# Copying and accumulating the output projection's weight sums: each pair tied to an attention or retention norm, on GpSimd's queue

## The chip, the cores and the metric

The kernel runs on one core of a Trainium2 chip. The metric is device time in microseconds (us) of one execution. Before the change it is 1619.31 us, the median of 3 runs (1617.8 to 1620.54).

## What is computed

One layer of a decoder trunk for 256 tokens and 2048 channels, all in float32. Cut to what matters:

```python
h = rms_norm(x, ln1_g)
aq, ak, av, iq, ik, iw, rq, rk, rv, rg, ga, gb = split(h @ w_in)
o_attn = sparse_attention(rms_norm(aq), rms_norm(ak), av, top 64 keys by indexer(iq, ik, iw))
o_ret = silu(rg) * group_norm(retention(rotate(rq), rotate(rk), rv))
merged = sigmoid(ga) * (o_attn @ w_up_attn) + sigmoid(gb) * (o_ret @ w_up_ret)
x = x + merged @ w_out
x = x + square(relu(rms_norm(x) @ w_ff1)) @ w_ff2
```

Every weight is read once from HBM. The two norms that matter here are the head norms of `ak` and of the four parts of `aq`, and the group norms of the four parts of the retention.

## The kernel before

**Matrix products.** The weights come in blocks of 512 columns (368 for the indexer's), each block in parts of 4 x 128 rows: 1 MB for 512 columns. A part is loaded into one of four `raw` buffers (`load`, L380, SP's queue). `split_now` makes two pieces of each half of a part: a high one, `whi`, on ScalarE (L429) and the remainder, `wlo`, on VectorE (L430). `products` (L495 to L497) runs three matmuls per 128 rows and token tile: high by high, high by low, low by high. A half of a part is thus 12 matmuls, a part 24. A `raw` buffer comes free when the last `wlo` of its part is made, and only then is the next load issued on SP's queue.

**Order of the work.** `program()` lists all halves of parts in order: first `AK` and the indexer's block `I 0` together, then `I 1`, `I 2`, `AV`, four blocks `AQ`, two of `RV`, then the gates' blocks, then four blocks `RG` (the retention runs beside them), `UR`, the output projection and the feed-forward part. `weights()` moves on by one item and calls `ahead()`, which issues loads and splits for later items. Work that is not a weight product (indexer, norms, softmax, transposes) lies in Python generators that `step()` advances by one `yield` for every 128 rows of products. A scheduler then orders the instructions of each engine; the order is fixed when the program is built.

**Strassen's form and the sums in DRAM.** Some products are made by a seven-product scheme on quarters A, B, C, D of a weight matrix, which needs sums of quarters. For the output projection `w_out`, half of its weights are formed ahead of time in four DRAM tensors `pre`: A+B, B+C, C+(A+B) and D+(C+A+B). Each tensor has two halves of 1 MB, so there are eight pairs of DMAs: a **copy** of a quarter from the weights into `pre` (`nc.sync.dma_start`, L453, SP's queue), and an **accumulation** of the second quarter, or of an earlier `pre`, onto it (`accum_op=ALU.add`, L451, GpSimd's queue). The table `background` says at which item of `program()` each is issued: copies at items 22, 31, 40, 49, 58, 67, and the last two pairs at the first item of `RG` and nine later; the accumulation 8 items after its copy. The copies depend on nothing, so the scheduler was free to put them earlier. The first reader of `pre` is a load at L380 at 829.4 us.

**GpSimd's queue** (POOL in the profile) executes in order and holds: the power in `rsqrt` (L507) of every norm, the accumulations, the stores of the gates' results (`keep`, L793), accumulations into `raw` (L437), and in the retention the loads of its values (`rvs`, L970), of the group norm's gains (`mid`, L972) and of the stored gates (`got`, L994, L998). A DMA on it that has to wait for another DMA makes everything behind it on POOL wait.

**The norms.** `head_norm_T` makes the norm of a block: squares, sums, then `rsqrt`, which is a VectorE operation (L506) and a power on POOL (L507); after a `yield`, VectorE scales the rows. `retain` makes the retention of two heads, its statistics (L949, L950), then `rsqrt` and an offset `off` on VectorE (L954), and ScalarE normalizes with both (L959). `small` tiles are the few columns that hold such factors.

Of the kernel before, what the change touches and what calls it, by code (L numbers as in the profile page):

```python
# [14 lines left out]
ALU = mybir.AluOpType  # L15
# [3 lines left out]
D = 2048  # L19
# [13 lines left out]
KC, HC = 4, 2  # L33
# [79 lines left out]
HK = DK // 2  # L113
# [64 lines left out]
def program():  # L178

    out = [(z, h, s) for h in range(DK // KC) for s in range(KC // HC) for z in (("AK", 0), ("I", 0))]  # L180
    for key in [("I", 1), ("I", 2), ("AV", 0)] + [("AQ", i) for i in range(4)] + [("RV", 0), ("RV", 1)]:
        out += block(key)
    out += gates()
    for i in range(4):
        out += block(("RG", i))
    out += [(z, h, s) for h in range(DK // KC) for s in range(KC // HC) for z in (("UR", 0), ("UR", 1))]
    out += second_half()
    out += block(("F1", 1), NORM_COLS) + block(("F1", 0))
    for g in range(1, NG):
        out += merged(g)  # L190
    return out + [("F2", NG - 1, i, h, s) for i in range(D // BN) for h in F2_HALVES for s in range(KC // HC)]
# [17 lines left out]
def block_kernel(ctx, tc, cst, rot, xt, gains, w, x, ret_gn_g, ret_gn_b, out):  # L209
    nc = tc.nc  # L210
# [16 lines left out]
    def nm(s):  # L227
        uid[0] += 1
        return f"{s}_{uid[0]}"
# [20 lines left out]
    def small(w):  # L250
        return sp.tile([P, w], F32, tag="small", name=nm("small"), bufs=n_sm)
# [47 lines left out]
    at, B, base, off = {}, {}, {}, 0  # L299
# [12 lines left out]
    use = program()  # L312

    pre = {z: dp.tile([HK // KC, P, KC * BN + 16], F32, name=nm("pre"))[:, :, :KC * BN].rearrange("h p (c n) -> h p c n", c=KC) for z in QUARTERS}
    formed = set()
    for n, p in enumerate(OUT_ORDER):
        z = PRODUCTS[p][1]
        for h in range(HK // KC):
            at[("OQ", n), h] = (pre[z][h] if p in (1, 2, 4, 6) else base[z, h], BN)
    background = {}  # L320
    late_at = use.index((("RG", 0), 0, 0))
    paced = [22 + 9 * j for j in range(6)] + [late_at, late_at + 9]
    for j, (z, two) in enumerate((("A", "B"), ("B", "C"), ("C", "A"), ("D", "C"))):
        for h in range(HK // KC):
            i = paced[2 * j + h]
            background[i] = (pre[z][h], base[z, h], False)
            background[i + 8] = (pre[z][h], base[two, h] if j < 2 else pre[two][h], True)

    def tile_of(item):
        if item[0] == "Q" and item[1] == OUT:  # L330
            return ("OQ", item[2]), item[3]
        if item[0] == "Q":
            return (PRODUCTS[ORDER[item[2]]][1], item[1], item[3]), 0
        if item[0] == "F2":
            return item[:4], 0
        return item if item[0] in BESIDE else item[:2]
# [18 lines left out]
    next_load, next_split, now, quarter, second_w, n_second = [0], [0], [0], [0], [0], [0]  # L355

    def ring(key):
        if key in BESIDE:
            return 3
        return 2 if key[0] == "F2" and key[1] < NG - 1 else 0  # L360
# [41 lines left out]
    def split(i):  # L402
        if first_gate - 16 <= i <= last_gate or first_out - 4 <= i <= last_out + 6:
            with tc.high_priority(offset=AHEAD):
                split_now(i)
        else:
            split_now(i)
# [32 lines left out]
    def room(i):  # L440
        key = loads[i][0]
        if key[0] in QUARTERS and "f2" not in late:
            return False
        n = ring(key)
        return not n or ("rawc" in late and second_w[0] - (n_second[0] // HT if key[0] == "F2" else n_second[0]) < n)

    def ahead(i):
        if i in background:
            d, a, add = background[i]
            if add:  # L450
                nc.gpsimd.dma_start(d, a, accum_op=ALU.add)  # L451
            else:
                nc.sync.dma_start(d, a)  # L453
        for _ in range(2):
            while next_load[0] < len(loads) and first_use[next_load[0]] <= i + LOAD_AHEAD and room(next_load[0]):
                load(next_load[0])
                next_load[0] += 1
            while next_split[0] < min(len(use), i + SPLIT_AHEAD + ("f1" in late or "fourth" in late) + 1):
                n_second[0] += ring(tile_of(use[next_split[0]])[0]) > 0
                split(next_split[0])  # L460
                next_split[0] += 1
# [41 lines left out]
    def rsqrt(v, n, mul):  # L503

        a, y = small(n), small(n)
        nc.vector.tensor_scalar(a, v, mul, EPS, op0=ALU.mult, op1=ALU.add)  # L506
        nc.gpsimd.tensor_tensor(y, a, half[:, :n], op=ALU.pow)  # L507
        return y
# [55 lines left out]
    def head_norm_T(rows, dsts, g, wait):  # L564

        hs = small(4 * T)
        for t, a in enumerate(rows):
            sq = stage()
            nc.scalar.activation(sq, a, AF.Square)
            nc.vector.tensor_reduce(hs[:, 4 * t:4 * t + 4], sq.rearrange("p (h d) -> p h d", h=4), axis=AX.X, op=ALU.add)  # L570
        yield
        r = rsqrt(hs, 4 * T, 1.0 / HD)
        yield
        for t, a in enumerate(rows):
            av = a.rearrange("p (h d) -> p h d", h=4)
            nc.vector.tensor_tensor(av, av, r[:, 4 * t:4 * t + 4].unsqueeze(2).to_broadcast([P, 4, HD]), op=ALU.mult)
        for _ in range(wait):
            yield
        for t, a in enumerate(rows):
            pst = psum_t()  # L580
            for h in range(4):
                nc.tensor.transpose(pst[:, h * P:(h + 1) * P], a[:, h * P:(h + 1) * P], ident)
            src = pst.rearrange("p (h i) -> p h i", h=4)
            if dsts[t][0] is not None:
                nc.scalar.activation(dsts[t][0], src, AF.Copy, scale=g)
            if len(dsts[t]) > 1:
                hi, lo = dsts[t][1:]
                nc.scalar.activation(hi, src, AF.Copy, scale=g)
                nc.vector.scalar_tensor_tensor(lo, src, g, hi.bitcast(F32), op0=ALU.mult, op1=ALU.subtract)
            yield  # L590
# [289 lines left out]
    for item in gates():  # L880
# [14 lines left out]
        if key == "UA":  # L895
            for t in range(T):
                a = stage()
# [27 lines left out]
    def retain(j, sg, rv, gb):  # L925
        h0 = 2 * j
        yield
        for a in range(2):
            k, q = rkT[:, h0 + a], rqT[:, h0 + a]
            ps = psum_a()  # L930
            nc.tensor.matmul(ps[:, :S], k[:, :P], q, start=True, stop=True)
            nc.tensor.matmul(ps[:, S:S + P], k[:, P:], q[:, P:], start=True, stop=True)
            z = stage()[:, :S + P]
            nc.vector.tensor_tensor(z[:, :S], ps[:, :S], dec[:, h0 + a].rearrange("p b i -> p (b i)"), op=ALU.mult)
            nc.vector.tensor_tensor(z[:, S:], ps[:, S:S + P], dec[:, h0 + a, 0], op=ALU.mult)
            nc.scalar.activation(am[:, 0, a], z, AF.Copy)
            nc.vector.tensor_tensor(am[:, 1, a], z, am[:, 0, a].bitcast(F32), op=ALU.subtract)
            yield
        yield
        yield  # L940
        psy, mv = [psum_a() for _ in range(T)], small(4 * T)
        for t in range(T):
            for a in range(2):
                c = slice(a * RV, (a + 1) * RV)
                for n, (x, i) in enumerate(((0, 0),) if t == 0 else ((2, 1), (1, 0))):
                    products([psy[t][:, c]], [z[:, i, c] for z in rv], [[am[:, b, a, x * P:(x + 1) * P] for b in range(2)]], n == 0, n == t)
            for a in range(2):
                st = small(6)
                nc.vector.bn_stats(st, psy[t][:, a * RV:(a + 1) * RV])  # L949
                nc.vector.bn_aggr(mv[:, 4 * t + 2 * a:4 * t + 2 * a + 2], st)  # L950
            yield
        mean, var = (mv.rearrange("p (a b) -> p a b", b=2)[:, :, i] for i in range(2))
        r, off = rsqrt(var, 2 * T, 1.0), small(2 * T)
        nc.vector.scalar_tensor_tensor(off, mean, -1.0, r, op0=ALU.mult, op1=ALU.mult)  # L954
        for t in range(T):
            y = stage()
            for a in range(2):
                c, i = slice(a * RV, (a + 1) * RV), 2 * t + a
                nc.scalar.activation(y[:, c], psy[t][:, c], AF.Identity, bias=off[:, i:i + 1], scale=r[:, i:i + 1])  # L959
            yield  # L960
            nc.vector.tensor_tensor(y, y, gb[0], op=ALU.mult)
            nc.vector.tensor_tensor(y, y, gb[1], op=ALU.add)
            nc.vector.tensor_tensor(y, y, sg[t], op=ALU.mult)
            yield
            work.append(transpose_in(rT, 4 * j, t, y, W_GN))

    for j in range(4):
# [8 lines left out]
        for t in range(T):  # L976
            z = mid([P, BN])
# [331 lines left out]
```

## Time and profile before

| | before |
|---|---|
| Time, median of 3 runs | 1619.31 us |
| Profiled execution's own time | 1618.96 us |
| Its span | 1616.9 us |
| PE busy | 1597.2 us, 99% of the span, 7370 matmuls |
| PEld (weight loads of TensorE) busy | 1322.6 us |
| DVE busy | 1326.8 us |
| ACT busy | 1039.5 us |
| POOL busy | 131.1 us |
| Moved by DMA | 391.65 MB, mean 242 GB/s |

PE is TensorE's matmuls, PEld its weight loads, DVE VectorE, ACT ScalarE, POOL GpSimd, SP the SyncE, which only issues DMAs. All times are microseconds from the span's start. Matmuls overlap, so a row's duration is longer than the distance to the next start, and PE counts as busy nearly always; what a stall costs is read from the distance between starts. "DMA share" is the mean busy share of the core's 16 DMA engines; q1 is the queue of SP's DMAs, q0 that of GpSimd's. A DMA's "us to landing" runs from its issue to its completion. PEclk is the TensorE clock that was granted, as a share of full speed.

### The profile page before, as it was taken

Reading aid. Unit: us, or ns where it says so; the run is one execution under the profiler, and the core shown is the slowest. Engines: PE = TensorE matmul, PEld = TensorE weight load, DVE = VectorE, ACT = ScalarE, POOL = GpSimd, SP = SyncE. Lnnn points to the kernel's source line nnn. Section 1 sums busy time; section 2 is a strip of 40 time slices with the busy share of each in tenths; the row PEclk is TensorE's granted clock in tenths of the full one; section 3 lists DMA queues with packets and bytes.
Section 4 is the critical chain, followed back from the end, with each engine's and each line's share of the span. In section 5 each row is a group of like instructions: output and inputs, shape, how many; then the busy total and the mean of one; then the engine's idle time right before and its main releaser. Section 6 shows DMA issues by size and latency. Waiting matters only on the chain.

```text
span 1616.9 us, 19794 instructions
## 1 busy us (share of the span) xinstructions
PE 1597.2 (99%) x7370; PEld 1322.6 (82%) x7370; DVE 1326.8 (82%) x1380; ACT 1039.5 (64%) x1290; POOL 131.1 (8%) x177
## 2 busy tenths in 40 slices
PE   9998999999999999999999999999999999999998
PEld 8976888888888888888878878888888888888887
DVE  6576877989989899687777789898989898989884
ACT  6553657666767676454556786766777676767672
POOL 0100000100100000111110000010000000000000
PEclk9999999999999999999999999999999999999999
DMA  9999447979788684874767874768676777777773
GB/s 328 291 329 298 153 142 259 308 256 310 242 291 266 226 264 155 294 249 164 285 234 287 305 268 177 237 208 258 201 242 209 236 232 234 234 234 230 217 205 129
DMA packets 78928, 391.65 MB, mean 242 GB/s; under 512 B 8944, under 2 KB 15728, under 8 KB 42864
## 3 DMA queue, kind: packets, MB, share of 16 engines
q1 hardware_dynamic: 58240, 326.00, 55.0%
q0 software_dynamic: 17856, 58.21, 16.6%
q10 hardware_dynamic: 2736, 6.18, 1.0%
q8 instruction: 58, 0.95, 0.2%
q14 instruction: 38, 0.31, 0.0%
HBM read 360.99 MB, written 46.14 MB: 252 GB/s over the span
## 4 chain that ended last, share of the span: by engine, by line
PE 92%; DMA 3%; DVE 3%; ACT 1%; issue 1%; SPq 0%; DVEq 0%; ACTq 0%
PE pm L497 12%; PE pm L496 12%; PE pm L495 12%; PE pq L495 10%; PE pq L496 10%; PE pq L497 10%; PE pf L495 7%; PE pf L497 7%; PE pf L496 7%; DMA raw<-in_w_dram 3%; DVE wlo L430 1%; PE pt L524 1%; ACT whi L429 1%; PE pa L495 0%; PE pa L496 0%
## 5 line engine op out<-in xcount | busy, mean ns | idle before, releaser
L430 DVE TENSOR_TENSOR wlo<-raw,whi 128x1024 fp32r<-128x1024 f32 (+2 forms) x568 | 675.0, 1203 | 188.9 <-ACT whi L429 179.4
L429 ACT ACTIVATE whi<-raw 128x1024 fp32r<-128x1024 f32 (+2 forms) x568 | 587.8, 1042 | 371.0 <-PE pm L497 196.4
L495 PE MATMUL pm<-whi,act 128*128 128x512 f32 (+1 forms) x928 | 360.1, 389 | 6.0 <-ACT whi L429 6.0
L496 PE MATMUL pm<-wlo,act 128*128 128x512 f32 (+1 forms) x928 | 357.9, 386 | 2.9 <-DVE wlo L430 2.9
L497 PE MATMUL pm<-whi,act 128*128 128x512 f32 (+1 forms) x928 | 357.2, 385 | 0.0
L430 DVE TENSOR_TENSOR wlo<-rawc,whi 128x1024 fp32r<-128x1024 f32 x176 | 214.8, 1221 | 41.4 <-ACT whi L429 39.5
L429 ACT ACTIVATE whi<-rawc 128x1024 fp32r<-128x1024 f32 x176 | 186.6, 1060 | 84.8 <-PE pf L497 23.2
L495 PEld LDWEIGHTS pm<-whi,act 128*128 128x128 f32 x928 | 174.7, 188 | 39.0 <-ACT whi L429 7.9
L496 PEld LDWEIGHTS pm<-wlo,act 128*128 128x128 f32 x928 | 174.8, 188 | 36.8 <-DVE wlo L430 6.2
L497 PEld LDWEIGHTS pm<-whi,act 128*128 128x128 f32 x928 | 174.7, 188 | 32.8
L495 PE MATMUL pf<-whi,act 128*128 128x512 f32 x512 | 200.0, 391 | 0.2 <-ACT whi L429 0.2
L497 PE MATMUL pf<-whi,act 128*128 128x512 f32 x512 | 199.5, 390 | 0.0
L496 PE MATMUL pf<-wlo,act 128*128 128x512 f32 x512 | 199.3, 389 | 0.0
L417 DVE TENSOR_TENSOR raw<-raw,raw 128x2048 f32<-128x2048 f32 x86 | 196.6, 2286 | 0.8
L495 PE MATMUL pq<-whi,xf 128*128 128x512 f32 x416 | 163.6, 393 | 0.0
L496 PE MATMUL pq<-wlo,xf 128*128 128x512 f32 x416 | 162.2, 390 | 0.0
L497 PE MATMUL pq<-whi,xf 128*128 128x512 f32 x416 | 162.1, 390 | 0.0
L497 PEld LDWEIGHTS pf<-whi,act 128*128 128x128 f32 x512 | 96.1, 188 | 20.1
L495 PEld LDWEIGHTS pf<-whi,act 128*128 128x128 f32 x512 | 96.0, 188 | 20.1 <-ACT whi L429 0.6
L496 PEld LDWEIGHTS pf<-wlo,act 128*128 128x128 f32 x512 | 96.2, 188 | 19.9
L1255 POOL DMA_DIRECT2D sums<-ev x56 | 49.1, 967 | 577.5 <-ACT ev L1254 577.0
L497 PEld LDWEIGHTS pq<-whi,xf 128*128 128x128 f32 x416 | 78.1, 188 | 16.3
(223 smaller groups left out, 1718.8 us busy)
## 6 DMA issues: line engine op xcount, KB each, us to landing
raw<-in_w_dram SPq DMA_DIRECT2D x186, 1024.0 KB, 7.0
rawc<-in_w_dram SPq DMA_DIRECT2D x56, 1024.0 KB, 6.5
rawc<-in_w_dram SPq DMA_DIRECT2D x64, 512.0 KB, 5.9
sums<-ev POOLq DMA_DIRECT2D x56, 256.0 KB, 5.5
raw<-in_w_dram POOLq DMA_DIRECT2D x10, 1024.0 KB, 9.8
pre<-in_w_dram SPq DMA_DIRECT2D x8, 1024.0 KB, 18.5
raw<-pre SPq DMA_DIRECT2D x8, 1024.0 KB, 5.7
raw<-in_w_dram SPq DMA_DIRECT2D x8, 736.0 KB, 6.1
```

Source lines behind the costliest of these rows:

```text
L417: nc.vector.tensor_tensor(one, one, two, op=ALU.add)
L429: nc.scalar.activation(a, src, AF.Copy)
L430: nc.vector.tensor_tensor(b, src, a.bitcast(F32), op=ALU.subtract)
L495: nc.tensor.matmul(d, h, hi, start=first, stop=False, skip_group_check=skip)
L496: nc.tensor.matmul(d, h, lo, start=False, stop=False, skip_group_check=skip)
L497: nc.tensor.matmul(d, l, hi, start=False, stop=last, skip_group_check=skip)
L524: nc.tensor.transpose(ps[:, c * P:(c + 1) * P], src[:, c * P:(c + 1) * P], ident)
L1255: nc.gpsimd.dma_start(sums[:, t, i * BN:(i + 1) * BN], z, accum_op=ALU.add)
```

## The change

The table of fixed places is replaced by a function `pace(mark)`, called at nine norms: right after `rsqrt` in `head_norm_T` (one call for `AK`, four for `AQ`), and after `off` in `retain` (four calls, of which the first three find a pair left). Each call takes the next of the eight pairs in the same order as before and issues on GpSimd's queue: a DMA of one element of the norm's result into the first element of the target in `pre`, then the copy of the quarter over the same target. Because both write the same bytes, the copy waits for the one-element DMA, and that one for the norm; so the scheduler can't put the copy earlier. The accumulation follows, again 8 items later in `program()` and on GpSimd's queue.

```diff
     background = {}
-    late_at = use.index((("RG", 0), 0, 0))
-    paced = [22 + 9 * j for j in range(6)] + [late_at, late_at + 9]
-    for j, (z, two) in enumerate((("A", "B"), ("B", "C"), ("C", "A"), ("D", "C"))):
-        for h in range(HK // KC):
-            i = paced[2 * j + h]
-            background[i] = (pre[z][h], base[z, h], False)
-            background[i + 8] = (pre[z][h], base[two, h] if j < 2 else pre[two][h], True)
+    pairs = [(z, two, h) for z, two in (("A", "B"), ("B", "C"), ("C", "A"), ("D", "C")) for h in range(HK // KC)]
+
+    def pace(mark):
+
+        if pairs:
+            z, two, h = pairs.pop(0)
+            d = pre[z][h]
+            nc.gpsimd.dma_start(d[0:1, 0, 0:1], mark[0:1, 0:1])
+            nc.gpsimd.dma_start(d, base[z, h])
+            background[now[0] + 8] = (d, base[two, h] if z in "AB" else pre[two][h])
...
     def ahead(i):
         if i in background:
-            d, a, add = background[i]
-            if add:
-                nc.gpsimd.dma_start(d, a, accum_op=ALU.add)
-            else:
-                nc.sync.dma_start(d, a)
+            d, a = background[i]
+            nc.gpsimd.dma_start(d, a, accum_op=ALU.add)
...
         r = rsqrt(hs, 4 * T, 1.0 / HD)
+        pace(r)
         yield
...
         nc.vector.scalar_tensor_tensor(off, mean, -1.0, r, op0=ALU.mult, op1=ALU.mult)
+        pace(off)
         for t in range(T):
```

The order of PE, DVE and ACT is the same in both programs, instruction for instruction. Lines of the changed program are numbered 2 or 3 higher below the table.

SP's queue in the indexer's blocks, where `raw` are the weight loads in their order of use and `pre_123` to `pre_126` are the sums of A, B, C and D. Before:

```order
L380 DMA raw_563<-in_w_dram 128x4x368
L453 DMA pre_123<-in_w_dram 128x2048
L380 DMA raw_597<-in_w_dram 128x4x368
L453 DMA pre_123<-in_w_dram 128x2048
L380 DMA raw_647<-in_w_dram 128x4x368
L380 DMA raw_685<-in_w_dram 128x2048
L453 DMA pre_124<-in_w_dram 128x2048
```

The same place of SP's queue with the change:

```order
L383 DMA raw_565<-in_w_dram 128x4x368
L383 DMA raw_599<-in_w_dram 128x4x368
L383 DMA raw_648<-in_w_dram 128x4x368
L383 DMA raw_686<-in_w_dram 128x2048
L383 DMA raw_721<-in_w_dram 128x2048
```

The eight copies have left SP's queue, and the weight loads stand there one behind the other.

POOL's queue in the attention, from the norm of `AK` (`small_536`) to that of the second `AQ` block. Before:

```order
L507 TENSOR_TENSOR small_536<-small_535,half 128x8
L451 DMA pre_123<-in_w_dram 128x2048 x2
L451 DMA pre_124<-in_w_dram 128x2048 x2
L451 DMA pre_125<-pre_123 128x2048 x2
L451 DMA pre_126<-pre_125 128x2048 x2
L507 TENSOR_TENSOR small_1331<-small_1330,half 128x8
L507 TENSOR_TENSOR small_1594<-small_1593,half 128x8
```

With the change (L328 is the one-element DMA, L329 the copy, L453 the accumulation):

```order
L507 TENSOR_TENSOR small_536<-small_535,half 128x8
L328 DMA pre_123<-small_536 1x1
L329 DMA pre_123<-in_w_dram 128x2048
L453 DMA pre_123<-in_w_dram 128x2048
L507 TENSOR_TENSOR small_1328<-small_1327,half 128x8
L328 DMA pre_123<-small_1328 1x1
L329 DMA pre_123<-in_w_dram 128x2048
L453 DMA pre_123<-in_w_dram 128x2048
L507 TENSOR_TENSOR small_1592<-small_1591,half 128x8
```

All eight accumulations stood ahead of the norm of the first `AQ` block; now one pair does, and one more follows each of the four `AQ` norms.

POOL's queue at the last pair, around the norm of the retention's third part (`small_6236`, with the change `small_6240`): `mid` are gains of the group norm, `got` the stored gates. Before:

```order
L972 DMA mid_6116<-in_ret_gn_g_dram 128x512
L972 DMA mid_6117<-in_ret_gn_b_dram 128x512
L507 TENSOR_TENSOR small_6236<-small_6235,half 128x4
L994 DMA got<-ga 128x512
L994 DMA got<-ua 128x512
```

With the change:

```order
L974 DMA mid_6120<-in_ret_gn_g_dram 128x512
L974 DMA mid_6121<-in_ret_gn_b_dram 128x512
L507 TENSOR_TENSOR small_6240<-small_6239,half 128x4
L328 DMA pre_126<-small_6243 1x1
L329 DMA pre_126<-in_w_dram 128x2048
L453 DMA pre_126<-pre_125 128x2048
L996 DMA got<-ga 128x512
L996 DMA got<-ua 128x512
```

A pair now stands between that norm and the loads of the stored gates; the norm of the fourth part (at 770.46 us in the profile before) comes behind them.

## The prediction

> **What bounds the kernel now.** I read the page first: its span and the line of DMA shares.
>
> ```profile
> span 1616.9 us, 19794 instructions
> DMA  9999447979788684874767874768676777777773
> ```
>
> The second line has 40 slices of 40.4 us. The first four are full, to about 160 us, and the next two at four tenths. So I asked for the busy times in stretches. Columns: stretch, its length, busy time of PE, PEld, DVE, ACT, POOL with instructions in brackets, granted clock, DMA share, GB/s.
>
> ```profile
> 50.00:78.00 28.00, 25.61 (x155) 25.01 (x155) 13.53 (x16) 12.24 (x18) 2.87 (x3) 1.00 0.99 301
> 78.00:110.00 32.00, 32.00 (x188) 26.30 (x188) 21.38 (x37) 18.64 (x27) 2.44 (x3) 1.00 1.02 356
> 110.00:142.00 32.00, 26.15 (x112) 19.30 (x109) 25.06 (x74) 11.47 (x15) 2.44 (x3) 0.98 1.02 297
> 160.00:255.00 95.00, 95.00 (x482) 78.91 (x481) 75.33 (x121) 61.23 (x127) 4.91 (x3) 1.00 0.41 145
> 680.00:765.00 85.00, 85.00 (x428) 72.19 (x427) 65.84 (x113) 40.92 (x56) 10.47 (x16) 1.00 0.56 198
> ```
>
> PE is full except in 50 to 142 us, where the DMA engines are full. The chain of waits passes there through two weight loads, one of 17.05 and one of 27.91 us (start, length, what):
>
> ```profile
> 57.88 17.05 DMA raw<-in_w_dram
> ...
> 76.86 0.44 PE pm L496
> ...
> 110.58 27.91 DMA raw<-in_w_dram
> ```
>
> What fills the engines, by the tile view of `pre` (median issue time, first and last start) and the DMA view (median us to landing; first of 110 to 140 us, then of 160 to 255 us):
>
> ```profile
> L453 SPq DMA_DIRECT2D pre<-in_w_dram x8: 496/530/621, 49.8 to 101.7; - x8
> L451 POOL DMA_DIRECT2D pre<-in_w_dram x4: 812/815/1065, 57.0 to 95.1; - x4
> L451 POOL DMA_DIRECT2D pre<-pre x4: 812/813/817, 107.6 to 136.5; - x4
> ```
> ```profile
> raw<-in_w_dram SPq DMA_DIRECT2D x4, 1024.0 KB, 22.1
> pre<-pre POOLq DMA_DIRECT2D x3, 1024.0 KB, 14.6
> ```
> ```profile
> raw<-in_w_dram SPq DMA_DIRECT2D x14, 1024.0 KB, 4.8
> ```
>
> All 16 transfers of `pre` are issued from 49.8 to 136.5 us. Beside them a weight load takes 22.1 us, without them 4.8. The timeline of PE shows where that reached it:
>
> ```profile
> 73.71 0.33 PE L497 MATMUL pm<-whi,act 128*128 128x368 f32 x1
> 75.90 0.43 PE L495 MATMUL pm<-whi,act 128*128 128x368 f32 x1 [1.86 <-ACT whi L429]
> ```
> ```profile
> 127.96 0.39 PE L496 MATMUL pm<-wlo,act 128*128 128x512 f32 x1
> 128.19 0.39 PE L497 MATMUL pm<-whi,act 128*128 128x512 f32 x1
> ...
> 130.97 0.50 PE L496 MATMUL pm<-wlo,act 128*128 128x512 f32 x1 [0.75 <-DVE wlo L430]
> ```
> ```profile
> 136.28 0.39 PE L497 MATMUL pm<-whi,act 128*128 128x512 f32 x1
> 139.70 0.50 PE L495 MATMUL pm<-whi,act 128*128 128x512 f32 x1 [3.04 <-ACT whi L429]
> 140.96 0.79 PE L496 MATMUL pm<-wlo,act 128*128 128x512 f32 x1 [0.76 <-DVE wlo L430]
> ```
> ```profile
> 140.80:144.20 3.40, 3.24 (x8) 2.56 (x9) 3.37 (x8) 2.93 (x5) 0.00 (x0) 0.50 1.01 277
> ```
>
> Matmuls of 512 columns start 0.23 us apart when nothing is missing (127.96, 128.19), those of 368 columns about 0.17. Three times PE waits for `whi` and then for `wlo` of a part that has just landed, and after the longest wait its clock is granted at 0.50 for 3.40 us (last row).
>
> **Part 1, the early stretch without seven of the pairs.** What stops there:
> - First stall: from 73.71 to 76.86 PE starts two matmuls, 3.15 us less 2 x 0.17 = 2.81 us.
> - Second: 128.19 to 130.97, 2.78 - 2 x 0.23 = 2.32 us. Third: 136.28 to 140.96, 4.68 - 0.46 = 4.22 us. Together 6.54.
> - Clock: 3.40 us at half speed, 1.70 us.
>
> If these waits go, VectorE is late next: in 110 to 142 it carries the indexer.
>
> ```profile
> 121.63 1.21 DVE L430 TENSOR_TENSOR wlo<-raw,whi 128x1024 fp32r<-128x1024 f32 x1
> 124.52 1.21 DVE L430 TENSOR_TENSOR wlo<-raw,whi 128x1024 fp32r<-128x1024 f32 x1
> 129.70 1.22 DVE L430 TENSOR_TENSOR wlo<-raw,whi 128x1024 fp32r<-128x1024 f32 x1 [2.19 <-ACT whi L429]
> 139.68 1.23 DVE L430 TENSOR_TENSOR wlo<-raw,whi 128x1024 fp32r<-128x1024 f32 x1 [4.16 <-ACT whi L429]
> ```
>
> Unhindered it makes a `wlo` every 2.89 us (121.63, 124.52), PE uses one up in 12 x 0.23 = 2.76. So PE stays behind VectorE there, and the second and third stall give back what VectorE idled, 2.19 + 4.16 = 6.35 us, not 6.54. The sum of part 1: 2.81 + 6.35 + 1.70 = 10.9 us (10.86).
>
> Does the first stall really go? Its load, issued at 57.88, had to share with copies and two accumulations; with the change, one copy and one accumulation are left from about 52 to 75 us. By the queue rows of 112 to 130 us (packets, MB, share of the 16 engines in 18 us) an accumulation costs 0.658 x 18 / 2.37 = 5.0 us of all engines per MB, a plain transfer 0.355 x 18 / 2.36 = 2.7:
>
> ```profile
> q0 software_dynamic: 321, 2.37, 65.8%
> q1 hardware_dynamic: 321, 2.36, 35.5%
> ```
>
> A pair is thus about 7.7 us of DMA time per MB, 8.1 for its 1.05 MB. Of the work ahead of that load at least one copy (2.8 us) and part of the second accumulation (5.3) leave, and it was late by 2.0 us (73.71 to 75.90, less 0.17). It lands in time, with some 4 us in hand.
>
> **Part 2, the seven pairs at their new places.** Four follow the `AQ` norms, three the retention's. POOL's timeline (start, length, operation, idle time ahead and its releaser) and who ends the quiet after:
>
> ```profile
> 147.77 1.66 POOL L507 TENSOR_TENSOR small<-small,half 128x8 f32<-128x8 f32 x1 [10.47 <-DVE small L506]
> 174.38 1.64 POOL L507 TENSOR_TENSOR small<-small,half 128x8 f32<-128x8 f32 x1 [24.95 <-DVE small L506]
> ```
> ```profile
> 738.40 1.03 POOL L507 TENSOR_TENSOR small<-small,half 128x4 f32<-128x4 f32 x1 [18.16 <-DVE small L506]
> 762.77 0.59 POOL L994 DMA_DIRECT2D got<-ga  x1 [23.34 <-PE pa L497]
> ```
> ```profile
> 770.46 1.18 POOL L507 TENSOR_TENSOR small<-small,half 128x4 f32<-128x4 f32 x1
> ```
>
> DMA time: 160 to 255 us is 0.41 x 95 = 39 us busy; four pairs add 32, in all 71 of 95. 680 to 765 is 0.56 x 85 = 48; three pairs add 24, in all 72 of 85. Both fit. A load may also be slow without harm: the one of 27.91 us stalled PE by 139.70 - 136.28 - 0.23 = 3.2 us, so one under some 24 us costs nothing in these blocks. With one pair in flight I expect 10 to 16. Taken: 0.
>
> POOL's own order: a pair holds POOL until its copy has landed, because the accumulation behind it waits. Nearest rows, for the one-element DMA the smallest one, for the copy one that SP issued in the quiet at 49.8 us and, as the upper end, the accumulations into `raw`, for the accumulation the first and the late ones (12.3, and 14.6 above):
>
> ```profile
> gT<-in_gains_dram ACTq DMA_DIRECT2D x1, 17.0 KB, 2.5
> ```
> ```profile
> pre<-in_w_dram SPq DMA_DIRECT2D x1, 1024.0 KB, 6.9
> ```
> ```profile
> raw<-in_w_dram POOLq DMA_DIRECT2D x10, 1024.0 KB, 9.8
> ```
> ```profile
> pre<-in_w_dram POOLq DMA_DIRECT2D x2, 1024.0 KB, 12.3
> ```
>
> POOL is held 2.5 + 6.9 to 9.8, some 10 to 12 us with the 0.81 us that an issue takes. The next `AQ` norm comes 174.38 - 147.77 = 26.6 us later, so nobody waits. At the last pair the norm starts at 738.40; its accumulation lands 1.03 + 2.5 + 6.9 + 12.3 = 22.7 us later, at 761, or at worst 1.03 + 2.5 + 9.8 + 14.6 = 27.9 later, at 766. The loads of the stored gates start at 762.77 on the same queue, and the fourth norm (770.46) stands behind them. So 0 to 4 us at the norm; since VectorE's and ScalarE's work lies between it and PE, I take 0.5. The issues themselves (16 one-element DMAs and copies x 0.81 = 13 us of POOL) lie in POOL's idle time. Less than nothing can't come from part 2: it only adds work.
>
> A rule that speaks against the change: the Trainium skill, "DMA: Bandwidth & Descriptors", section "Issuing engines are not separate DMA queues", says that DMAs from SP, ScalarE and GpSimd end on the same 16 engines and that another issuing engine saves only issue time. By it alone, moving the queue would be worth SP's issue time, and all else must come from the later time. This case's rows for q0 and q1 agree, since both share the same percentages.
>
> **The sum.** 1618.96 (the profiled execution's own time, 2.06 more than its span) - 10.9 + 0.5 = 1608.6. The median of the runs is 0.35 above that execution: 1608.9. No change means within 0.2%, 3.2 us, about what a measurement of this kernel can tell.
>
> **The rivals.**
> - *The last pair delays the fourth retention norm* (16%). The accumulation lands at 766 rather than 761, the loads of the stored gates queue behind it, and PE waits for the transposes of the normalized rows. For it: little slack, 1.8 us between 761 and 762.77. Price 2 to 4 us: 1611 to 1613. The same would follow if VectorE kept POOL from issuing: three issues, each longer by up to a `wlo`, 1.2 us, are 3.6 us more, at the same price. Against that part: with VectorE 78% busy in 110 to 142 us (25.06 of 32), issues of L451 took 0.81 us, at most 1.07. The Trainium skill, "SBUF — State Buffer", section "SBUF: two separate sides", states such a mechanism: while VectorE runs a two-port operation, GpSimd can't write its DMAs' descriptors. The rows of L451 show no such hold-up.
> - *The first pair still holds the load of 73 us* (8%). It is the one pair that stays early. Then 2.8 us less gain: 1611.7.
> - *Slower: both halves of each pair squeeze the weights* (4%). Beside accumulations q1 moved 2.36 MB in 18 us, 0.131 MB per us; PE uses 1.05 MB in 24 x 0.23 = 5.5 us, 0.19. If copies on GpSimd's queue behaved so too, each pair would squeeze for 25 of 26.6 us, 1.5 MB or 8 us of PE. Four pairs make 32 us; the slack of a load covers 24 - 4.8 = 19, 13 remain. Three retention pairs: 24 - 19 = 5. 1608.6 + 18 = 1627. It decides once loads take over 24 us in these blocks. Against it: in 78 to 110 five copies and three accumulations ran in 32 us, and PE was full.
> - *The tie doesn't hold* (4%): the copies go out early anyway or the indexer's VectorE work takes the place of the stalls; the time stays within 3 us of 1619. Against it: the copy writes bytes that the one-element DMA wrote before it, and VectorE's idle rows above.
>
> **How the numbers follow.** The forecast itself has 68%: all stalls gone, nothing new beyond 0.5 us, 1607.2 to 1610.5. The low end, 1606.8, is 1608.9 less 0.5 and less the scatter of a median (1.5). The high end takes in the first two rivals: 1613. Together 92%, less some for sizes that I mis-set. Faster by over 0.2%: 0.68 + 0.16 + 0.08 = 0.92; within: 0.04; slower: 0.04.
>
> **What would show it.** In the changed profile: of the transfers of `pre` only one pair before 130 us; DMA share in 80 to 140 us at half or less; weight loads of about 5 us there; no idle time of PE over 0.5 us between 70 and 145 us; the clock at 1.00 throughout it. In the `AQ` blocks, DMA share near 0.75 and PE full. At the last pair, the first load of the stored gates no later against the third norm than 24.4 us (762.77 - 738.40). Wrong would be: a PE wait for `whi` in the `AQ` or `RG` blocks, a `pre` copy over 12 us, or a third retention norm's accumulation that lands more than 26 us behind it.

## The result and the profile after

The changed kernel takes 1608.61 us (median of 4 runs, 1606.32 to 1610.49) against 1618.67 us before (4 runs, 1617.8 to 1620.54): ratio 0.9936, interval 0.9918 to 0.9953. That is 0.64% faster; 1608.9 was forecast. The profiled execution took 1607.76 us.

From the page of the changed kernel, the span and the DMA share in 40 slices of 40.1 us:

```profile
span 1605.6 us, 19809 instructions
DMA  9847578978878675798767874767686767777763
```

The span is 11.3 us shorter. Slices three and four, full before, read four and seven; slices five and six, four before, read five and seven. The same bytes move at other times. The stretches, with the columns as in the prediction:

```profile
50.00:78.00 28.00, 28.00 (x172) 27.86 (x171) 16.06 (x18) 14.63 (x20) 2.78 (x4) 1.00 0.89 294
78.00:110.00 32.00, 32.00 (x186) 25.62 (x185) 22.22 (x43) 19.23 (x28) 0.00 (x0) 1.00 0.45 156
110.00:142.00 32.00, 31.84 (x139) 24.98 (x138) 29.63 (x76) 14.66 (x16) 2.27 (x2) 1.00 0.51 183
160.00:255.00 95.00, 94.13 (x470) 77.99 (x469) 73.38 (x111) 57.70 (x110) 13.17 (x16) 1.00 0.70 230
680.00:765.00 85.00, 85.00 (x420) 71.85 (x418) 65.81 (x109) 42.28 (x57) 18.97 (x29) 1.00 0.90 287
```

PE is full in 50 to 142 us but for 0.16 us, the clock stays at 1.00, and the DMA share there falls to about a half, where it was 1.02. The new places carry the load: 0.70 where it was 0.41, 0.90 where it was 0.56, and PE stays full in the second. (The 0.87 us that PE lacks in 160 to 255 is the wait at 246.28 below, which stood at 257.61 before, outside this stretch.)

The tile view of `pre`: one-element DMA, copy, and the accumulations of the first four and of the last four pairs, with the first and last start:

```profile
L328 POOL DMA_DIRECT2D pre<-small x8: 587/602/737, 50.9 to 728.5; - x8
L329 POOL DMA_DIRECT2D pre<-in_w_dram x8: 534/542/574, 54.0 to 732.4; - x8
...
L453 POOL DMA_DIRECT2D pre<-in_w_dram x4: 841/849/860, 61.1 to 204.1; - x4
L453 POOL DMA_DIRECT2D pre<-pre x4: 853/868/872, 232.8 to 738.2; - x4
```

The tie holds: the copies run from 54.0 to 732.4 us, where they ran from 49.8 to 101.7. The DMA view of 78 to 142 us, then of 160 to 260 us (KB each, median us to landing):

```profile
raw<-in_w_dram SPq DMA_DIRECT2D x11, 1024.0 KB, 4.8
```
```profile
raw<-in_w_dram SPq DMA_DIRECT2D x13, 1024.0 KB, 6.2
```

Weight loads in the indexer's blocks take 4.8 us (22.1 before). Beside one pair at a time, in the `AQ` blocks, they take 6.2.

**Where the 11.3 us came from.** PE's order is the same in both kernels, so one and the same matmul can be compared. The rows show the matmul that starts at 73.71 us before, the last one ahead of the first stall, and a late one of the attention, at 256.34 before, first in the changed kernel and then in the kernel before:

```profile
73.35 0.33 PE L497 MATMUL pm<-whi,act 128*128 128x368 f32 x1
...
116.17 0.39 PE L495 MATMUL pm<-whi,act 128*128 128x512 f32 x1
116.71 0.50 PE L496 MATMUL pm<-wlo,act 128*128 128x512 f32 x1 [0.16 <-DVE wlo L433]
...
245.01 0.40 PE L497 MATMUL pq<-mid,vv 128*128 128x512 f32 x1
246.28 0.50 PE L495 MATMUL pq<-mid,vv 128*128 128x512 f32 x1 [0.87 <-ACT mid L734]
```
```profile
256.34 0.40 PE L497 MATMUL pq<-mid,vv 128*128 128x512 f32 x1
```

73.71 - 73.35 = 0.36 us lie ahead of everything that the change touches; 256.34 - 245.01 = 11.33. So 10.97 us came between 73 and 256 us, and matmul by matmul all of it by 146 us. From there to the end the two run in step (11.3 of the spans), but for some 1.1 us that the changed kernel gains at 800 us and loses again by 940. The wait for `wlo` at 116.71 is the one small wait that is left in the indexer; before, it ended at 120.00.

The last pair, by POOL's timeline and the DMA view of 735 to 745 us:

```profile
727.01 1.03 POOL L507 TENSOR_TENSOR small<-small,half 128x4 f32<-128x4 f32 x1 [10.00 <-DVE small L506]
...
738.15 0.87 POOL L453 DMA_DIRECT2D pre<-pre  x1 [5.19 <-DMA pre<-in_w_dram]
751.38 0.59 POOL L996 DMA_DIRECT2D got<-ga  x1 [12.36 <-PE pa L497]
```
```profile
pre<-pre POOLq DMA_DIRECT2D x1, 1024.0 KB, 8.1
```

The accumulation lands 738.15 + 8.1 - 727.01 = 19.2 us behind its norm, and the loads of the stored gates start 24.4 us behind it, as before. The loads of the stored gates wait for PE there, not for the pair.

### The profile page after: what moved, and what is told of

Same layout as the page of the kernel before. It is cut to its first block, busy times and chain, and to the rows that moved or that the text cites. A ratio compares the mean times of both kernels' runs of the same rounds, so it can differ in the third digit from the quotient of the medians.

```text
span 1605.6 us, 19809 instructions
## 1 busy us (share of the span) xinstructions
PE 1595.3 (99%) x7370; PEld 1322.6 (82%) x7370; DVE 1326.0 (83%) x1380; ACT 1040.9 (65%) x1290; POOL 141.3 (9%) x193
## 4 chain that ended last, share of the span: by engine, by line
PE 95%; DVE 3%; ACT 1%; issue 0%; DMA 0%; SPq 0%; DVEq 0%; ACTq 0%
PE pm L496 13%; PE pm L497 13%; PE pm L495 13%; PE pq L496 10%; PE pq L497 10%; PE pq L495 10%; PE pf L495 7%; PE pf L497 7%; PE pf L496 7%; DVE wlo L433 1%; PE pt L524 1%; DVE mid L651 1%; ACT whi L432 0%; PE pa L495 0%; PE pa L496 0%
```

## The experiments

**Theory** as in the prediction: the gain is the later time, since the DMA engines were full from 50 to 142 us. **Rival**: the gain is the queue, since no copy stands ahead of a weight load on SP's queue any more. Each ratio is to the kernel before, measured beside it.

**Queue without time: all eight pairs at the norm of `AK`.**

```diff
         r = rsqrt(hs, 4 * T, 1.0 / HD)
-        pace(r)
+        if wait == 2 * W_NORM:
+            for _ in range(8):
+                pace(r)
...
-        pace(off)
```

The accumulations follow one item apart, 8 to 15 items later.

> All eight pairs at the early place, but on GpSimd's queue and tied to the norm of AK: the queue is the changed kernel's, the time nearly that of before. Theory (the gain is the later time, because the DMA engines are full from 50 to 142 us): no gain, 1616 to 1624 us, PE stalls between 70 and 160 us, DMA share near 1.0 there; POOL may hold the first AQ norm a little longer than before. Rival (the gain is that no copy stands in front of a weight load on SP's queue): 1612 us or less, the stalls mostly gone.

Measured: 1617.85 us, ratio 1.0007 (0.9997 to 1.0017): no gain. PE's timeline, two stretches, and the weight loads of 78 to 142 us:

```profile
73.59 0.32 PE L497 MATMUL pm<-whi,act 128*128 128x368 f32 x1
77.22 0.68 PE L495 MATMUL pm<-whi,act 128*128 128x368 f32 x1 [3.31 <-ACT whi L432]
```
```profile
80.00:90.00 10.00, 9.34 (x43) 8.23 (x42) 3.08 (x5) 4.44 (x7) 2.57 (x4) 0.82 1.01 367
110.00:142.00 32.00, 31.85 (x143) 24.56 (x142) 30.21 (x83) 14.12 (x17) 1.61 (x2) 1.00 1.03 282
```
```profile
raw<-in_w_dram SPq DMA_DIRECT2D x10, 1024.0 KB, 19.5
```

The total fits the theory, but the time is not lost where it was lost before, so that the totals agree is chance. Compared matmul by matmul with the changed kernel, PE loses 7.7 us up to 86 us: the first stall is longer than before, and the clock drops behind it (0.82 on average in 80 to 90). Some 3 us more go between 142 and 158 us, where PE waits for rows of the first `AQ` block (longest 0.80 us at 149.85 and 0.84 at 157.56, both for VectorE); what made those late is not shown. In 110 to 142 us, with the engines full (1.03) and loads at 19.5 us, PE is as full as in the changed kernel: the second and third stall of before are gone. Full engines alone didn't stall PE there, and for that stretch the run speaks for the rival.

**Time without queue: the copies tied, but on SP's queue.**

```diff
-            nc.gpsimd.dma_start(d, base[z, h])
+            nc.sync.dma_start(d, base[z, h])
```

> The changed kernel with the eight copies issued on SP's queue again, each behind the one-element DMA that ties it to its norm: the time is the changed kernel's, the queue that of before. Theory (time): as the changed kernel within 2 us, 1607 to 1611 us. Rival (queue): the gain goes, 1615 us or more, with weight loads that wait behind a copy on SP's queue.

Measured: 1607.24 us, ratio 0.9937 (0.9924 to 0.9950), the changed kernel's. With the later time the queue is worth nothing that can be measured.

**Only the accumulations late.** The copies stand in the old table on SP's queue; `pace` issues the one-element DMA and puts the accumulation 8 items later.

```diff
-            background[i + 8] = (pre[z][h], base[two, h] if j < 2 else pre[two][h], True)
+            pairs.append((pre[z][h], base[two, h] if j < 2 else pre[two][h]))
...
+            d, a = pairs.pop(0)
+            nc.gpsimd.dma_start(d[0:1, 0, 0:1], mark[0:1, 0:1])
+            background[now[0] + 8] = (d, a, True)
```

> Copies as before (SP's queue, early), only the accumulations tied to the norms; the one-element DMA here overwrites one element of each copied half, so one weight of each is not the quarter's. Theory, by the price per MB (5.0 us of all engines for an accumulation, 2.7 for a copy): the seven accumulations are two thirds of what filled the engines; with the eight copies and one accumulation left, 50 to 142 us is about 60% full, weight loads take 8 to 10 us and no stall is left: 1607 to 1611 us. Rival (the copies ahead of the loads on SP's queue did it): 1614 us or more.

Measured: 1608.24 us, ratio 0.9939 (0.9927 to 0.9951): the whole gain. Two stretches and the loads of 78 to 142 us:

```profile
78.00:110.00 32.00, 32.00 (x187) 25.66 (x186) 22.16 (x41) 19.54 (x29) 0.00 (x0) 1.00 0.92 360
110.00:142.00 32.00, 31.85 (x140) 24.96 (x139) 29.66 (x79) 14.53 (x17) 2.28 (x2) 1.00 0.53 190
```
```profile
raw<-in_w_dram SPq DMA_DIRECT2D x10, 1024.0 KB, 5.2
```

All eight copies still stand among the loads, and the loads take 5.2 us in the median, since by 110 us the copies are through (0.53 after it). Early on the engines were fuller than expected: 0.94 in 50 to 78 us and 0.92 in 78 to 110, where about 0.6 was said for the whole stretch. With the accumulations gone, at 5.0 us of all engines per MB against 2.7, the copies no longer reach the stretch of the second and third stall.

**No pairs at all.** `at[("OQ", n), h]` reads `base[z, h]` for every product, and the table `background` stays empty.

> No copies and no accumulations at all: the output projection reads single quarters where it should read sums of quarters, so that part of the computation is left out. It shows what the pairs cost at their new places. Theory (nothing, PE is full there): the changed kernel's time within 1.5 us, 1607 to 1609.5 us, so about 0.65% under before. Rival (the new places cost some us that the sum missed): 1605 us or less.

Measured: 1608.08 us, ratio 0.9939 (0.9927 to 0.9951). A kernel without one copy or accumulation is no faster than the changed one, so the pairs cost nothing that can be measured at their new places.

**No pair at the norm of `AK`.**

```diff
-        pace(r)
+        if wait != 2 * W_NORM:
+            pace(r)
```

> The changed kernel without the pair at the norm of AK: pairs one to four at the AQ norms, five to eight at the four retention norms. It shows what the one pair that stayed early costs. Theory (its weight load lands in time): the changed kernel's time within 1 us, 1607.5 to 1609.5 us. Rival (that pair still holds something up): 1606.5 us or less.

Measured: 1607.97 us, ratio 0.9941 (0.9927 to 0.9955). The one pair that stayed early costs nothing either.

**All eight pairs at the four `AQ` norms**, two at each, the second accumulation 12 items later.

```diff
-        pace(r)
+        if wait != 2 * W_NORM:
+            pace(r)
+            pace(r)
```

> All eight pairs at the four AQ norms, two at each. Measured in the changed kernel, four pairs took the DMA share in 160 to 255 us from 0.41 to 0.70, 6.9 us a pair; eight make 39 + 55 = 94 of 95 us. Theory (loads may take up to 24 us before PE waits): the engines are full but PE keeps most of its time, 1608 to 1613 us, loads of 10 to 20 us. Rival (PE stalls as soon as the engines are full, as it did early): 1615 us or more, with a clock that drops again.

Measured: 1609.38 us, ratio 0.9951 (0.9939 to 0.9964). The stretch of the `AQ` blocks, and the loads of 150 to 245 us:

```profile
160.00:255.00 95.00, 94.13 (x471) 78.00 (x470) 73.32 (x112) 58.12 (x111) 18.89 (x25) 1.00 0.96 298
```
```profile
raw<-in_w_dram SPq DMA_DIRECT2D x13, 1024.0 KB, 11.4
```

The engines are full (0.96), loads take 11.4 us, and PE is as full in this stretch as in the changed kernel. That is the second place where full engines stall nothing. They are not quite free: the time is 1.4 us above the kernel without the pair at `AK`, measured beside it (1607.97). In its profile, PE loses 1.6 us just behind the stretch (287.70 to 289.52, less 0.23), waiting for a `wlo`. VectorE is 3.8 us late there, against the changed kernel, after waits for `whi` of up to 5.0 us (2.9 in the changed kernel). (The 6.9 us a pair in this expectation is too low; the price is worked out again below.)

**The last three pairs at the third retention norm.**

```diff
-        pace(off)
+        if j == 2:
+            for _ in range(3):
+                pace(off)
```

The accumulations follow 8, 9 and 10 items later.

> The last three pairs all at the third retention norm, so that POOL and its queue are held until after the loads of the stored gates should start, and the fourth norm comes late. It sizes the first rival of the prediction. If that rival's mechanism is right: the last accumulation lands some 40 us behind the norm, the fourth norm comes 10 to 15 us later, and PE waits about as long less the slack: 1615 to 1623 us. If the work behind that norm has slack: under 1611 us.

Measured: 1619.98 us, ratio 1.0014 (1.0005 to 1.0023): the gain is gone, 11 us. POOL, VectorE and PE around it:

```profile
753.47 0.80 POOL L453 DMA_DIRECT2D pre<-pre  x1 [10.89 <-DMA pre<-pre]
...
770.80 1.18 POOL L507 TENSOR_TENSOR small<-small,half 128x4 f32<-128x4 f32 x1
```
```profile
767.52 0.69 DVE L1001 TENSOR_TENSOR got<-got 128x512 f32<-128x512 f32 x1 [13.94 <-DMA got<-ua]
768.13 1.22 DVE L433 TENSOR_TENSOR wlo<-raw,whi 128x1024 fp32r<-128x1024 f32 x1
```
```profile
759.54 0.39 PE L495 MATMUL pm<-whi,act 128*128 128x512 f32 x1
769.40 0.79 PE L496 MATMUL pm<-wlo,act 128*128 128x512 f32 x1 [9.47 <-DVE wlo L433]
```

The accumulations hold the queue, the loads of the stored gates land late, and VectorE stands 13.94 us at the product of those gates with a `wlo` queued behind it. PE waits 9.47 us for that `wlo`, and its clock is granted at 0.54 for the 3.40 us from 769.80. The fourth norm comes at 770.80 us, 12 us later than in the changed kernel (758.62), as expected, but PE's wait is not for it.

**Untied: the kernel before with its copies on GpSimd's queue.**

```diff
             else:
-                nc.sync.dma_start(d, a)
+                nc.gpsimd.dma_start(d, a)
```

> The kernel before with its copies moved to GpSimd's queue by one word, and no tie. The scheduler then puts seven of the eight pairs ahead of the first norm on POOL. If the tie is what carries the change: slower than before, by 40 us or more, because the first norm waits on POOL until pairs have landed while the DMA engines are full with the first loads. If the queue alone were worth something: faster than before.

Measured: 1661.28 us (2 runs), ratio 1.0269 (1.0249 to 1.0289). The first norm on POOL, and PE's waits of 0 to 110 us (total, times, longest):

```profile
90.16 0.72 POOL L507 TENSOR_TENSOR small<-small,half 128x2 f32<-128x2 f32 x1 [31.60 <-DVE small L506]
```
```profile
PE pm L495 <- ACT whi L429: 32.1, 8, 7.8
```

The copies start at 1.29 us and meet the first loads. PE waits 32.1 us for `whi`, and the clock is granted at 0.83 in 0 to 50 us and at 0.64 in 50 to 78; the norm comes at 90.16 us and not at 40.66 because its sums come late, not because POOL holds it (the row names VectorE). Of the two reasons expected, only the DMA load was shown.

**A refined theory.** After these runs the theory needed a change: PE waits where a weight load takes longer than its buffers give it, and not where the engines are full. Two kernels test that: seven (then five) pairs tied to the transposed query tiles of the indexer at 80 to 90 us. Of the calls at the norms only that of `AK` is left (with five, also those of the retention), and an accumulation whose item is taken goes to the next free one.

```diff
             nc.scalar.activation(iqT[:, c:c + 2, :], ps.rearrange("p (a s) -> p a s", a=2), AF.Copy)
+            for _ in range(2):
+                pace(iqT[:, c, :])
```

> One pair at the norm of AK as in the changed kernel, the other seven tied to the indexer's four transposed query tiles, at about 80 to 90 us, on GpSimd's queue. So the DMA engines are full in 80 to 142 us again, as before, but no copy stands in front of a weight load on SP's queue, and the load that is needed at 73 us meets one pair alone. First theory (the gain is the later time: full DMA engines stall PE): 1614 us or more. Refined theory (PE waits only where a weight load takes longer than its buffers give it, 15 us in the indexer's blocks and 24 us in the next ones; behind pairs on another queue it takes 18 to 22 us): no wait for whi between 78 and 142 us although the DMA share is near 1.0; what remains is POOL, which holds the first AQ norm until the accumulations are issued, 0 to 4 us: 1608 to 1613 us.

Measured: 1626.81 us, ratio 1.0050 (1.0037 to 1.0063): slower, above what the refined theory said. The number lies in the first theory's "1614 us or more", but not for its reason, as the rows show. A stretch, the loads of 78 to 142 us, POOL and PE:

```profile
110.00:142.00 32.00, 31.06 (x133) 23.97 (x131) 26.55 (x72) 14.07 (x16) 1.61 (x2) 1.00 1.02 314
```
```profile
raw<-in_w_dram SPq DMA_DIRECT2D x10, 1024.0 KB, 11.7
```
```profile
148.09 0.80 POOL L456 DMA_DIRECT2D pre<-pre  x1 [28.53 <-DMA pre<-pre]
155.57 0.81 POOL L456 DMA_DIRECT2D pre<-pre  x1 [6.68 <-DMA pre<-pre]
156.12 1.96 POOL L510 TENSOR_TENSOR small<-small,half 128x8 f32<-128x8 f32 x1
```
```profile
140.82 0.39 PE L500 MATMUL pm<-whi,act 128*128 128x512 f32 x1
158.95 0.66 PE L587 MATMUL pt<-csb,stg 128*128 128x128 f32 x2 [17.74 <-DVE stg L581]
```

The part on the loads holds: engines full (0.92 in 78 to 110 us, 1.02 after it), no wait for `whi` up to 140.82 us. The loads take 11.7 us in the median, at most 21.1, less than the 18 to 22 that was said. The part on POOL was sized far too low: the last two accumulations wait 28.53 and 6.68 us for those that they read, the first `AQ` norm stands behind them, and PE waits 17.74 us for its rows.

With the last two pairs at the retention norms instead (`range(min(2, len(pairs) - 2))`):

> The same with five pairs at the indexer and the last two at the first two retention norms, so that POOL is free when the first AQ norm comes. Refined theory: the changed kernel's time within 1.5 us, 1607 to 1610 us. First theory in its strict form (each early pair costs its share of the stalls, 10.9 us for seven, so 1.5 us each): 1614 to 1617 us.

Measured: 1607.28 us, ratio 0.9930 (0.9916 to 0.9944), the changed kernel's. Its stretches and loads:

```profile
78.00:110.00 32.00, 32.00 (x187) 25.58 (x186) 22.16 (x43) 19.59 (x29) 7.78 (x13) 1.00 0.92 309
110.00:142.00 32.00, 31.85 (x139) 24.97 (x138) 29.66 (x76) 14.36 (x17) 3.28 (x3) 1.00 1.03 291
```
```profile
raw<-in_w_dram SPq DMA_DIRECT2D x10, 1024.0 KB, 11.7
```

Six of eight pairs are early here, the engines are as full as before the change (0.92 and 1.03), and the whole gain is there. Three things differ from before: no copy stands ahead of a load on SP's queue, two pairs are later, and the copies of the five pairs at the indexer start only at 86 us, so that the load needed at 73 us meets one pair. Which of the three carries how much is not separated here. The kernel with all eight pairs at `AK` says something on it: without copies on SP's queue the second and third stall are gone, and with five copies beside it the load of 73 us is late all the same.

## Why the prediction was right, point by point

- **Part 1, 10.9 us: right, in its places and waits too.** Measured 10.97 between 73 and 256 us. Of it 119.45 - 116.17 - 0.36 = 2.92 us fell before the small wait in the indexer (2.81 said), and 11.33 - 3.28 = 8.05 behind it (6.35 + 1.70 = 8.05 said). That the last two agree to the hundredth is luck: matmul by matmul the 8.05 are 2.30 and 4.23 us at the second and third stall, 6.53 and not 6.35, and 1.52 at the slow clock, not 1.70. That VectorE is late next was right: in the changed kernel it starts a `wlo` about every 2.9 us there (118.35, 121.23, 124.14), and the wait at 116.71 stayed. The load that the first stall waited for took 6.5 us, where it took 17.05 before, so it had more in hand than the 4 us said. None of the signs of being wrong came: PE never waits for `whi` in the `AQ` or `RG` blocks, and no copy took over 8.2 us.
- **Part 2, 0.5 us: too high, it is nothing that can be measured.** The kernel without pairs is no faster. The price of a pair was right. Its DMA time comes out of the stretch that holds all four pairs of the `AQ` blocks, in the changed kernel and in the kernel without pairs:

```profile
136.00:255.00 119.00, 118.13 (x594) 97.98 (x593) 91.41 (x139) 73.11 (x141) 16.82 (x20) 1.00 0.73 238
```
```profile
136.00:255.00 119.00, 118.13 (x595) 97.97 (x594) 91.27 (x139) 72.84 (x140) 8.95 (x8) 1.00 0.47 168
```

(0.73 - 0.47) x 119 / 4 = 7.7 us, where 8.1 was said. (The 6.9 above came from 160 to 255 us, which leaves out the first of the four: its accumulation was issued at 150.13 and took 9.2 us.) Loads there took 6.2 us, where 10 to 16 was said. An accumulation at the quiet place took 8.1 us and not 12.3, so the last one landed 19.2 us behind its norm, not 22.7 to 27.9.
- **What bounds the kernel: incomplete.** The prediction read "PE is full except in 50 to 142 us, where the DMA engines are full" as cause and effect. In three kernels the engines are as full (1.03 with all at `AK`, 0.96 in the `AQ` blocks, 1.03 with five at the indexer), and PE does not wait for weights in those stretches. What decides is how long a load takes. Before, the second and third stall wait for loads of 27.2 and 27.9 us; with all pairs at `AK`, loads of up to 21.8 us issued between 90 and 136 us stalled nothing. The limit lies between, where the prediction had put it for the third stall (24); for the load of 73 us it is about 15. Why the two loads took so long is seen in the kernel before, for the load and the copy issued between 101 and 102 us (median us to landing):

```profile
raw<-in_w_dram SPq DMA_DIRECT2D x1, 1024.0 KB, 27.2
pre<-in_w_dram SPq DMA_DIRECT2D x1, 1024.0 KB, 34.3
```

In this stretch SP's DMAs land in the order in which they were issued. The copy issued at 101.67 landed at 136.0, and the load issued behind it at 110.58 landed at 138.5, 27.91 us after its issue. So it waited for the copy, and the copy ran beside accumulations, which took 65.8% of the engines in 112 to 130 us (the row of q0 in the prediction). Later accumulations, or later pairs as a whole, each brought all loads under the limit. Copies off that queue alone did so for the second and third stall, and with the pairs also kept away from the load of 73 us, and two of them later, they did for all three. The number came out right since the change takes away both conditions, the copies ahead of the loads and the accumulations beside them.
- **First rival: a real danger, by another way.** Its threshold was not reached. With three pairs at one norm it is passed, and PE loses some 11 us, but not through the fourth norm: VectorE stands at the gates' product, with a `wlo` behind it.
- **Second rival: shown wrong** by the kernel without the pair at `AK`. **Third: wrong**, as loads in the `AQ` blocks stayed at 11.4 us in the median with twice the pairs. **Fourth: wrong**: the tie holds, and copies put on GpSimd's queue without it start at 1.29 us, for a time of 1661 us.
- **The rule of the Trainium skill**, "DMA: Bandwidth & Descriptors", section "Issuing engines are not separate DMA queues", by which another issuing engine saves only issue time: the copies tied on SP's queue agree with it (0.9937 against 0.9936), as long as they are late. In 110 to 142 us it did not hold alone: with all eight pairs at `AK` on GpSimd's queue and the engines as full (1.03), the second and third stall were gone. The prediction's remark that the rows for q0 and q1 "share the same percentages" reads them wrongly: they are 65.8% and 35.5%. What agrees with the rule is that they add up to 101% of the same 16 engines.

## What to carry to other kernels

Full DMA engines are no stall by themselves: compare how long a load takes with how long its buffers let it take, and ask what stands ahead of it on its queue. Work in DRAM that nobody needs soon can be tied by data to a result that comes when the DMA engines have room. Here it was then free, where its DMAs waited for each other with nothing urgent behind them on the same queue. An accumulation in DRAM is the expensive half of such a pair; moving that alone was enough here.

## What was not expected of the hardware

- A one-element DMA on GpSimd's queue took 1.6 us with the queue empty (median of 160 to 260 us in the changed kernel) and 15.7 to 15.9 us behind three copies of 1 MB (four of them in the kernel with seven pairs at the indexer): the tie costs as much as what stands ahead of it on its queue.
- The clock was granted at 0.5 for 3.40 us behind PE's 3.04 us of idle time, and stayed at 1.00 behind 1.86 and 1.14 us. With three pairs at one norm it was 0.54 for 3.40 us behind 9.47 us of idle time.
- With seven pairs at the indexer, an accumulation that reads what an earlier one wrote held POOL's queue for 28.53 us, where 1 MB of it costs 5.0 us of all DMA engines: the order on the queue cost far more than the bytes.
